# First feed-forward: the norm's root moves from the products into the inputs, which are split anew in place

## The chip, the cores and the metric

The kernel runs on one core of a Trainium2 chip. The metric is the device time of one execution in microseconds. A core has TensorE (PE, with its weight loads PEld), VectorE (DVE), ScalarE (ACT), GpSimd (POOL) and SyncE (SP, which issues most DMAs). Each takes its instructions in order and waits on semaphores where one needs another engine's result.

## The reference

Two layers of a streaming encoder over 1024 prompt frames and 64 sample frames, width 1024, all in fp32. Layer 0 mixes by sliding-window attention, layer 1 by an SSM. Behind each mixer comes a gated feed-forward with a causal convolution of width 3; the change lies in that of layer 0.

```python
def rms_norm(x, g):
    y = x32 * lax.rsqrt(jnp.mean(x32 * x32, axis=-1, keepdims=True) + NORM_EPS) * g
def conv_ffn(h, prev, w_up, conv_w, conv_b, w_down):       # D_FF = 2816
    up = h @ w_up
    full = jnp.concatenate([prev, up], axis=1)
    c = conv_b
    for j in range(CONV_WIDTH):
        c = c + conv_w[j] * full[:, j:j + t]
    return (jax.nn.gelu(c[..., :D_FF]) * c[..., D_FF:]) @ w_down, full[:, -(CONV_WIDTH - 1):]
...
    xp = xp + rms_norm(mp, g_post_mix[i])
    hp = rms_norm(xp, g_pre_ffn[i])
    fp, cpi = conv_ffn(hp, zeros, w_up[i], conv_w[i], conv_b[i], w_down[i])
    xp = xp + rms_norm(fp, g_post_ffn[i])
```

## The kernel before

Activations lie with features on partitions and the 1088 frames along the free dimension, in three blocks `b` of 384, 384 and 320 frames. Each fp32 product is made of three fp32r matmuls: an operand is split into a high part, rounded by a ScalarE copy, and a low part, the remainder by a DVE subtraction (`split`, L458; for weights `split_unit`, L213, into the tiles `whl`). `mm3` (L221 to L225) issues low times high, high times high and high times low.

`post_norm` leaves the residual sum of a block in a tile (`q` behind the attention, `y` elsewhere; the list `ys` in `build`), `pre_norm` (L293) splits that sum times the gain `g`, without the norm's root, into `hh` and `hl` (`h[b][0]`, `h[b][1]`), and puts the root, the same for all features of a frame, into `rb`. So the root is still missing in the products.

`ffn(i, ...)` computes the up-projection in 44 weight tiles of 128 features: tile `f` and tile `KF + f` (KF = 22) belong to one gate. `up_block` (L404) makes one block of a tile in 24 matmuls into one of six PSUM buffers `mm`, and evicts it into the tile's row `u`: by DVE with the factor `rb` (L414, L416), or, with `normed` set, by a ScalarE copy (L411, L412). The second feed-forward (i = 1) uses the copies from its fifth gate on, behind `normed(bs)` (L462), which multiplies `x[b]` in place by gain and root, and new splits of `h`. `conv` (L418) convolves `u` (one step on ScalarE, two on DVE), `gate` (L435) applies GELU, multiplies the two halves (L440) and stores the result to DRAM (`gd`).

The first tiles are computed as `us = up([0, KF, 1])`, block by block over the three; then `gate(0, us)`; then gates 1 to 21. Between the halves of each gate and behind it `aside` counts a turn (44 in all); it advances two side jobs: `sums`, which builds sums of `w_down` (`sums_w`) and of gates (`sums_g`) in the scratch tile `jt`, for the down-projection's block products, and `side`, the preparation of the SSM's tables (`ssm_prep`; its tiles `sm`, `kt`, `w`, and PE's `kps`, `wps` at L1072 and L1083). `jt` and two of the tables use slots that the residual sums held.

Weight tiles are loaded on SP's queue (`raw`, two buffers) and split two units ahead of their use (`AHEAD`) into six slots. The order on each engine is set by a scheduler that goes by priorities and estimated times, not by the order of the code alone; `order` adds fixed precedences on one engine, and `normed`'s products are put behind the last convolution step so far (`last_conv`).

Of the kernel before, what the change touches and what calls it, by code (L numbers as in the profile page):

```python
# [11 lines left out]
AF = mybir.ActivationFunctionType  # L12
# [6 lines left out]
SEQ, DEC, PAST = 1024, 64, 512  # L19
# [3 lines left out]
KF = DFF // P  # L23
# [3 lines left out]
SIDE = 32  # L27

PLAIN = 5
# [14 lines left out]
class Core:  # L44
# [295 lines left out]
    def ffn(self, i, h, rb, after, side=None, beside=lambda: None, x=None, g=None):  # L340

        nc, tc, a = self.nc, self.tc, self.a
# [10 lines left out]
        def sums_w(k):  # L353
            x = (jt[:, :2048] if i == 0 else self.yp.tile([P, 2048], F32, name="jw", tag="ypB", bufs=1)).rearrange("p (c h m) -> p c h m", c=2, h=2)
            Q.dma_start(x, a["w_down"][i, k::KH].rearrange("c p (h m) -> p c h m", h=2))
            yield
            a11, a12, a21, a22 = x[:, 0, 0], x[:, 1, 0], x[:, 0, 1], x[:, 1, 1]
            E.tensor_add(a22, a21, a22)
            E.tensor_sub(a21, a11, a21)
            E.tensor_sub(a11, a22, a11)  # L360
            E.tensor_sub(a12, a12, a11)
            Q.dma_start(sd[:, k], x)
# [14 lines left out]
            Q.dma_start(td[:, k], x)  # L377


        w0 = (PLAIN + 1) * i  # L380
        starts = {2 * (k + w0) + 1: sums_w(k) for k in range(KH)}
        starts.update({2 * (k + KH) + 2: sums_g(k) for k in range(KH)})
        jobs = {}
# [1 line left out]
        def sums(j):  # L385

            for x in jobs.pop(j, []):
                next(x, None)
            if j in starts:
                x = starts[j]  # L390
                next(x)
                jobs[j + 1 + i] = [x]
# [8 lines left out]
        def up_start(m):  # L401
            return self.unit(("w_up", i, m)), u_tile(m)

        def up_block(w, u, b, normed=False):  # L404
            t0, n = BLK[b]
            ps = self.mm_ps()
            for k in range(KD):
                self.mm3(ps[:, :n], w, slice(k * P, (k + 1) * P), h[b][0][:, k], h[b][1][:, k], k == 0, k == KD - 1)
            np_ = min(n, SEQ - t0)
            if normed:  # L410
                nc.scalar.activation(u[:, t0 + 2:t0 + 2 + np_], ps[:, :np_], AF.Copy)  # L411
                nc.scalar.activation(u[:, SEQ + 4:], ps[:, np_:n], AF.Copy)  # L412
                return
            nc.vector.tensor_mul(u[:, t0 + 2:t0 + 2 + np_], rb[:, t0:t0 + np_], ps[:, :np_])  # L414
            if np_ < n:
                nc.vector.tensor_mul(u[:, SEQ + 4:], rb[:, SEQ:], ps[:, np_:n])  # L416

        def conv(m, u):  # L418
# [5 lines left out]
            self.last_conv = nc.vector.scalar_tensor_tensor(t, u[:, 2:T + 4], cw(2, m), t, op0=ALU.mult, op1=ALU.add)  # L424
            return t

        def up(ms):

            wu = {m: up_start(m) for m in ms}
            for b in range(3):  # L430
                for w, u in wu.values():
                    up_block(w, u, b)
            return {m: u for m, (w, u) in wu.items()}

        def gate(f, us):  # L435
            ta = conv(f, us.pop(f) if f in us else up([f])[f])
            nc.scalar.activation(ta, ta, AF.Gelu_apprx_tanh)
            aside()
            tb = conv(KF + f, us.pop(KF + f) if KF + f in us else up([KF + f])[KF + f])
            nc.vector.tensor_mul(ta, ta, tb)  # L440
            Q.dma_start(gd[:, f, :SEQ], ta[:, :SEQ])
            Q.dma_start(gd[:, f, SEQ:], ta[:, SEQ + 2:])
# [3 lines left out]
        def aside():  # L446

            j = next(turns) + 1
            if side is not None and j <= SIDE:
                with self.later(LOW):  # L450
                    next(side, None)
            sums(j - 1)
# [43 lines left out]
        def seven(f, first):  # L496
# [11 lines left out]
            if first:  # L508
                up_block(w, ug, 2)
# [5 lines left out]
            if not first:  # L515
                up_block(w, ug, 2, True)
# [8 lines left out]
            up_block(w, uv, 2, not first)  # L525
            return {f: ug, KF + f: uv}

        us = up([0, KF, 1])
        gate(0, us)
        if i == 0:  # L530
            jt = self.yp.tile([P, 3072], F32, name="jt", tag="ypA", bufs=2)
        else:
            ts_ctx = tc.tile_pool(name="ts", bufs=1)
            ts = ts_ctx.__enter__()
            op = {}
        aside()
        for f in range(1, KF):
            if i == 1 and f == 2:
                normed((0, 1))
            if i == 1 and f == 3:  # L540
                late = input_sums()
            if i == 1 and f == PLAIN - 1:
                us = up([f, KF + f])
                into_place(*late)
                normed((2,))
            if i == 1 and f >= PLAIN:
                us = seven(f, f == PLAIN)
                if f == PLAIN:
                    for j in range(2):
                        split(half(h[2][0], j), half(h[2][1], j), half(x[2], j))  # L550
            if i == 0 and f == KF - 2:
                us = up([f, KF + f, f + 1])
            gate(f, us)
            aside()
# [961 lines left out]
def build(tc, a):  # L1516
    nc = tc.nc
    with ExitStack() as ctx:
        c = Core(ctx, tc, a)
        g = lambda j: c.pp[:, PPO["g"] + j * 8:PPO["g"] + j * 8 + 8]  # L1520
        cols = lambda v: [v[:, :, t0:t0 + n] for t0, n in BLK]
        xin = cols(a["x"])
        xd = [c.dram.tile([P, KD, T], F32, name=f"x{i}") for i in range(3)]
        h = []
        rb = c.t4([P, T], "rb")
        with c.boundary():
            xt = [c.bt(c.yp, b, "y") for b in range(3)]

            last = None
            for b in range(3):  # L1530
                step = 2 if b == 0 else 4
                for k in range(0, KD, step):
                    x = nc.sync.dma_start(xt[b][:, k:k + step], xin[b][:, k:k + step])
                    if last is not None:
                        c.order(x, last)
                    last = x
                    if (b, k) in ((0, 0), (0, 6), (1, 0)):
                        c.load_ahead(1 + len(c.ready))
                        c.order(c.loaded, last)
                        last = c.loaded  # L1540
            c.fill(c.mm_ps("idle"), 14, P)
            c.rest_of_pp()
            for b in range(3):
                h.append(c.pre_norm(xt[b], b, g(0), rb, first=b == 0))
        c.ssm_setup()

        def then(post, xs, xo, pre):

            nxt = [None] * 3
            rb, ys = [], []  # L1550

            def f(b, y):
                ys.append(y)
                c.post_norm(y, b, g(post), xs[b], post != 5 or b == 2, post in (3, 7), xo[b] if pre is None else None,
                            {3: "1111", 7: "0101"}.get(post) if b == 2 else None)()
                if pre == 4:
                    if b == 2:
                        c.ssm_bounce(y, b, [0])
                    c.ssm_norm(y, b)
                    if b == 2:  # L1560
                        c.ssm_bounce(y, b, range(1, 4), dict(c.sq))
                        c.spill = lambda: nc.sync.dma_start(xo[2], y)
                        return
                if pre is not None:
                    nc.sync.dma_start(xo[b], y)
                if pre in (2, 6) and b:
                    second(b - 1)
                    if b == 2:
                        second(2)

            def early():
                for b in range(2):
                    c.ssm_bounce(ys[b], b)

            def second(b):
                if b == 0:
                    rb.append(c.t4([P, T], "rb"))
                nxt[b] = c.pre_norm(ys[b], b, g(pre), rb[0], pre != 6 or b > 0)
            return f, nxt, rb, early, ys
        f, n1, r1, _, _ = then(1, xin, cols(xd[0]), 2)  # L1580
        c.attention(h, rb, f)
        f, _, _, early, _ = then(3, cols(xd[0]), cols(xd[1]), 4)
        c.ffn(0, n1, r1[0], f, c.ssm_prep(), early)
        f, n2, r2, _, ys = then(5, cols(xd[1]), cols(xd[2]), 6)
        c.ssm(f)
        f, _, _, _, _ = then(7, cols(xd[2]), cols(a["o_y"]), None)
        c.ffn(1, n2, r2[0], f, x=ys, g=g(6))
        c.close_ps()
# [21 lines left out]
```

## Time and profile before

| | us |
|---|---|
| runs | 2235.85, 2241.18, 2240.71 |
| median | 2240.71 |
| profiled execution, span | 2241.6 |
| PE busy | 2188.9 |
| DVE busy | 1687.4 |
| ScalarE busy | 1019.1 |
| POOL busy | 414.7 |

The page gives no time for the profiled execution beside its span, which is 0.9 us above the median. Busy times are sums over one engine; they overlap each other. Matmuls are pipelined and their ends are modelled, so a wait of PE is read from gaps and releasers, not from the share alone. A row of a group reads: line, engine, operation, output and inputs, shape, count, busy us in total, mean ns of one, idle time ahead of it and who ended it.

### The profile page before, as it was taken

To read this page: it belongs to the slowest core of one execution; us is meant where nothing else is said; L and a number is where in the kernel's file an instruction comes from. 1 tells how busy PE (TensorE), PEld (TensorE's weight loads), DVE (VectorE), ACT (ScalarE), POOL (GpSimd) and SP (SyncE) were. 2 spreads that over 40 slices of the span, in tenths; PEclk is the share of its full clock that TensorE was granted. 3 is DMA by queue.
4 is the path that set the end of the run, shared out by engine and by line. 5 is a ranking of instruction groups with operands and counts; after the bars stand their busy time and mean duration, and the time that the engine had idled before them with its cause. 6 is when DMAs were issued, how large, how long until landed. Compare 5 with 4: busy or idle time off the path is not lost.

```text
span 2241.6 us, 36077 instructions
## 1 busy us (share of the span) xinstructions
PE 2188.9 (98%) x13875; PEld 2114.0 (94%) x13875; DVE 1687.4 (75%) x2954; ACT 1019.1 (45%) x1839; POOL 414.7 (18%) x474
## 2 busy tenths in 40 slices
PE   9999999999999999999998899999999999999997
PEld 8987789999999999999996699999999999999997
DVE  8687648989877877666768865587997788786754
ACT  5256747422333333455534742263444444455543
POOL 5322004200042323100200034352011111110000
PEclk9999999999999999999999999999999999999999
DMA  5100015656345565887749998751266667678773
GB/s 197 38 22 29 20 62 158 246 184 211 111 136 183 181 192 184 253 298 232 229 147 340 272 295 297 261 167 65 96 217 223 236 237 276 209 269 310 224 243 99
DMA packets 208124, 428.48 MB, mean 191 GB/s; under 512 B 23312, under 2 KB 114224, under 8 KB 205008
## 3 DMA queue, kind: packets, MB, share of 16 engines
q1 hardware_dynamic: 175648, 326.56, 44.3%
q0 software_dynamic: 23984, 95.12, 11.9%
q10 hardware_dynamic: 8320, 4.49, 0.9%
q8 instruction: 109, 1.79, 0.3%
q14 instruction: 63, 0.52, 0.1%
HBM read 297.75 MB, written 128.37 MB: 190 GB/s over the span
## 4 chain that ended last, share of the span: by engine, by line
PE 47%; DMA 6%; DVE 5%; ACT 1%; issue 1%; SPq 1%; POOL 0%; DVEq 0%; ACTq 0%; POOLq 0%
PE mm L225 12%; PE mm L223 12%; PE mm L224 12%; DMA raw<-in_w_down 3%; PE pb L223 1%; PE pb L225 1%; PE pa L224 1%; PE pb L224 1%; PE pa L225 1%; PE pa L223 1%; DVE whl L216 1%; ACT whl L216 1%; DMA yd<-ys 1%; DMA pm<-prm 1%; DVE y L328 0%
## 5 line engine op out<-in xcount | busy, mean ns | idle before, releaser
L223 PE MATMUL mm<-hl,whl 128*128 128x384 f32 (+1 forms) x1960 | 643.4, 329 | 3.8 <-DVE hl L306 3.1
L225 PE MATMUL mm<-hh,whl 128*128 128x384 f32 (+1 forms) x1960 | 641.1, 328 | 2.2 <-DVE whl L216 2.2
L224 PE MATMUL mm<-hh,whl 128*128 128x384 f32 (+1 forms) x1960 | 642.3, 328 | 0.0
L223 PEld LDWEIGHTS mm<-hl,whl 128*128 128x128 f32 x1960 | 368.5, 188 | 6.0 <-DVE hl L306 4.5
L225 PEld LDWEIGHTS mm<-hh,whl 128*128 128x128 f32 x1960 | 368.5, 188 | 2.9 <-DVE whl L216 2.9
L224 PEld LDWEIGHTS mm<-hh,whl 128*128 128x128 f32 x1960 | 368.7, 188 | 0.0
L216 ACT ACTIVATE whl<-raw 128x1024 fp32r<-128x1024 f32 x202 | 212.9, 1058 | 333.4 <-PE mm L225 192.2
L216 DVE TENSOR_TENSOR whl<-raw,whl 128x1024 fp32r<-128x1024 f32 x202 | 254.9, 1264 | 111.2 <-ACT whl L216 110.7
L223 PE MATMUL mm<-gt,whl 128*128 128x384 f32 (+1 forms) x968 | 316.8, 327 | 2.6 <-ACT whl L216 1.7
L225 PE MATMUL mm<-gt,whl 128*128 128x384 f32 (+1 forms) x968 | 315.8, 327 | 0.7 <-DVE whl L216 0.7
L224 PE MATMUL mm<-gt,whl 128*128 128x384 f32 (+1 forms) x968 | 315.9, 327 | 0.0
L223 PEld LDWEIGHTS mm<-gt,whl 128*128 128x128 f32 x968 | 181.7, 188 | 3.2 <-ACT whl L216 1.9
L225 PEld LDWEIGHTS mm<-gt,whl 128*128 128x128 f32 x968 | 181.6, 188 | 1.2 <-DVE whl L216 1.2
L224 PEld LDWEIGHTS mm<-gt,whl 128*128 128x128 f32 x968 | 181.7, 188 | 0.0
L194 DVE TENSOR_TENSOR whl<-raw,whl 128x1024 fp32r<-128x1024 f32 x84 | 96.3, 1153 | 69.2 <-ACT whl L193 68.2
L193 ACT ACTIVATE whl<-raw 128x1024 fp32r<-128x1024 f32 x84 | 82.6, 987 | 115.0 <-DMA raw<-sd 50.2
L423 DVE SCALAR_TENSOR_TENSOR t<-u,ppt,t 128x1090 f32<-128x1090 f32 x88 | 123.6, 1407 | 7.9 <-ACT t L422 7.3
L422 ACT ACTIVATE t<-u,ppt 128x1090 f32<-128x1090 f32 x88 | 114.2, 1298 | 24.4 <-DVE u L521 9.2
L424 DVE SCALAR_TENSOR_TENSOR t<-u,ppt,t 128x1090 f32<-128x1090 f32 x88 | 123.3, 1403 | 0.4
L414 DVE TENSOR_TENSOR u<-rb,mm 128x384 f32<-128x384 f32 (+1 forms) x164 | 80.2, 502 | 20.4 <-PE mm L225 15.7
L566 DVE TENSOR_TENSOR gt<-gr,gt 128x768 fp32r<-128x768 f32 (+2 forms) x106 | 89.9, 879 | 7.1 <-ACT gt L565 6.8
L565 ACT ACTIVATE gt<-gr 128x768 fp32r<-128x768 f32 (+2 forms) x106 | 78.4, 773 | 35.6 <-DMA gr<-gd 24.6
(390 smaller groups left out, 4113.4 us busy)
## 6 DMA issues: line engine op xcount, KB each, us to landing
raw<-in_w_up SPq DMA_DIRECT2D x88, 512.0 KB, 4.2
raw<-in_w_down SPq DMA_DIRECT2D x74, 512.0 KB, 4.4
raw<-sd SPq DMA_DIRECT2D x40, 512.0 KB, 4.6
sj<-in_w_up POOLq DMA_DIRECT2D x68, 256.0 KB, 6.1
su<-sj POOLq DMA_DIRECT2D x34, 512.0 KB, 5.8
raw<-su SPq DMA_DIRECT2D x34, 512.0 KB, 4.7
pm<-prm SPq DMA_DIRECT2D x32, 522.0 KB, 8.6
gr<-td SPq DMA_DIRECT2D x40, 384.0 KB, 5.7
```

Source lines behind the costliest of these rows:

```text
L193: nc.scalar.activation(w[:, 0], raw, AF.Copy)
L194: nc.vector.tensor_sub(w[:, 1], raw, w[:, 0].bitcast(F32))
L216: x = nc.scalar.activation(w[:, 0], raw, AF.Copy), nc.vector.tensor_sub(w[:, 1], raw, w[:, 0].bitcast(F32))
L223: nc.tensor.matmul(out, w[:, 0, sl], xl, start=start, stop=False)
L224: nc.tensor.matmul(out, w[:, 0, sl], xh, start=False, stop=False)
L225: self.last_mm = nc.tensor.matmul(out, w[:, 1, sl], xh, start=False, stop=stop)
L414: nc.vector.tensor_mul(u[:, t0 + 2:t0 + 2 + np_], rb[:, t0:t0 + np_], ps[:, :np_])
L422: nc.scalar.activation(t, u[:, 0:T + 2], AF.Identity, bias=cb(m), scale=cw(0, m))
L423: nc.vector.scalar_tensor_tensor(t, u[:, 1:T + 3], cw(1, m), t, op0=ALU.mult, op1=ALU.add)
L424: self.last_conv = nc.vector.scalar_tensor_tensor(t, u[:, 2:T + 4], cw(2, m), t, op0=ALU.mult, op1=ALU.add)
L565: nc.scalar.activation(x[:, 0, u], raw, AF.Copy)
L566: nc.vector.tensor_sub(x[:, 1, u], raw, x[:, 0, u].bitcast(F32))
```

## The change

In the first feed-forward, behind gate 0, `normed(range(3))` multiplies all three residual sums in place by gain and root (24 DVE instructions). Tile KF + 1 is still computed from the old inputs. Then `resplit` writes `hh` and `hl` of all blocks anew from the multiplied sums, in halves of four features' groups (six ScalarE copies, six DVE subtractions), and from the next tile (2) on products are evicted by ScalarE copies without `rb`. The sums of `w_down` start two turns later, the SSM preparation one turn later, since their scratch tiles come free later.

```diff
-        w0 = (PLAIN + 1) * i
+        w0 = (PLAIN + 1) * i + (i == 0)
...
                 nc.scalar.activation(u[:, t0 + 2:t0 + 2 + np_], ps[:, :np_], AF.Copy)
-                nc.scalar.activation(u[:, SEQ + 4:], ps[:, np_:n], AF.Copy)
+                if np_ < n:
+                    nc.scalar.activation(u[:, SEQ + 4:], ps[:, np_:n], AF.Copy)
...
+        plain = [False]
+
         def up(ms):
             wu = {m: up_start(m) for m in ms}
             for b in range(3):
                 for w, u in wu.values():
-                    up_block(w, u, b)
+                    up_block(w, u, b, plain[0])
...
-            if side is not None and j <= SIDE:
+            if side is not None and 1 < j <= SIDE + 1:
...
+        def resplit():
+            for b in range(3):
+                for j in range(2):
+                    split(half(h[b][0], j), half(h[b][1], j), half(x[b], j))
+
         us = up([0, KF, 1])
         gate(0, us)
         if i == 0:
+            normed(range(3))
+            us.update(up([KF + 1]))
+            resplit()
+            plain[0] = True
             jt = self.yp.tile([P, 3072], F32, name="jt", tag="ypA", bufs=2)
...
-        f, n1, r1, _, _ = then(1, xin, cols(xd[0]), 2)
+        f, n1, r1, _, ys = then(1, xin, cols(xd[0]), 2)
...
-        c.ffn(0, n1, r1[0], f, c.ssm_prep(), early)
+        c.ffn(0, n1, r1[0], f, c.ssm_prep(), early, x=ys, g=g(2))
```

In the changed file the lines of `ffn` stand a little lower: L414 and L416 become L415 and L417, the convolution's DVE steps L423 and L424 become L424 and L425, the gate's product L440 becomes L443, `normed`'s product L470, `split` L462 and L463.

On DVE, at the first gate, before the change: the gate's product (L440) comes behind the sums in `jt`, and behind it the next convolution and the evictions of tile KF + 1 (`sm` belongs to the SSM's tables).

```order
L358 TENSOR_TENSOR jt<-jt 128x512 [waits DMAHW1_49]
L440 TENSOR_TENSOR t<-t 128x1090 [waits DVE_49]
L927 SCALAR_TENSOR_TENSOR sm_4272<-sm_4272 128x32 [waits DVE_49]
L359 TENSOR_TENSOR jt<-jt 128x512 [waits DVE_49]
L423 SCALAR_TENSOR_TENSOR t<-u,ppt,t 128x1090 [waits Activation_49]
L396 MEMSET u 128x2 [waits DVE_49]
L414 TENSOR_TENSOR u<-rb,mm 128x384 x2
L414 TENSOR_TENSOR u<-rb,mm 128x256
L416 TENSOR_TENSOR u<-rb,mm 128x64
```

On DVE at the same place after the change: the 24 products on `q` follow the second convolution step of tile KF, the gate's product stands among them, the evictions of KF + 1 behind them, and then the first four of the new splits.

```order
L470 SCALAR_TENSOR_TENSOR q<-q,ppt,rb 128x384 x8
L470 SCALAR_TENSOR_TENSOR q<-q,ppt,rb 128x384 [waits DMAHW0_49]
L470 SCALAR_TENSOR_TENSOR q<-q,ppt,rb 128x384 x4
L443 TENSOR_TENSOR t<-t 128x1090 [waits DVE_49]
L470 SCALAR_TENSOR_TENSOR q<-q,ppt,rb 128x384 x3
L470 SCALAR_TENSOR_TENSOR q<-q,ppt,rb 128x320 [waits DMAHW4_49]
L470 SCALAR_TENSOR_TENSOR q<-q,ppt,rb 128x320 x7
L396 MEMSET u 128x2
L415 TENSOR_TENSOR u<-rb,mm 128x384 x2
L415 TENSOR_TENSOR u<-rb,mm 128x256
L417 TENSOR_TENSOR u<-rb,mm 128x64
L463 TENSOR_TENSOR hl<-q,hh 128x1536 [waits Activation_49] x4
```

The sums in `jt` have left this place, and the products, and behind the evictions the splits, have come in; the convolution of tile 1 now stands behind the first four splits.

On PE, the end of tile KF + 1 (blocks of 320) and the start of tile 2, after the change; before it the rows are the same, but for the wait on ScalarE in the fourth.

```order
L224 MATMUL mm<-hh,whl 128x320
L225 MATMUL mm<-hh,whl 128x320
L223 MATMUL mm<-hl,whl 128x384 [waits DVE_49,PE_49]
L224 MATMUL mm<-hh,whl 128x384 [waits Activation_49]
L225 MATMUL mm<-hh,whl 128x384
```

Nothing moved on PE: tile 2 follows tile KF + 1 as before. Its first two matmuls now read the operands that DVE and ScalarE write anew.

On ScalarE, a little later, before the change (`cst` keeps the last columns of `u`):

```order
L398 COPY u<-ppt 128x2
L419 COPY cst<-u 128x4 [waits DVE_49]
L422 ACTIVATE t<-u,ppt 128x1090 [waits DVE_49,Activation_49]
L398 COPY u<-ppt 128x2 [waits DVE_49]
L216 ACTIVATE whl<-raw 128x1024 [waits DMAHW2_49,PE_49]
L437 ACTIVATE t<-t 128x1090 [waits DVE_49]
```

And after it, for tile 2:

```order
L411 ACTIVATE u<-mm 128x384 [waits PE_49] x2
L440 ACTIVATE t<-t 128x1090 [waits DVE_49]
L411 ACTIVATE u<-mm 128x256 [waits PE_49]
L413 ACTIVATE u<-mm 128x64
L216 ACTIVATE whl<-raw 128x1024 [waits DMAHW3_49]
L420 COPY cst<-u 128x4 [waits Activation_49]
```

The evictions have come to ScalarE, between GELU and the weight split.

## The prediction

> **What bounds the kernel now.** First the page's busy times and its chain, then the windows of the first feed-forward's up-projection (some 376 to 892 us), then what PE waits for there, then the timeline at the place that the change rewrites.
>
> ```profile
> PE 2188.9 (98%) x13875; PEld 2114.0 (94%) x13875; DVE 1687.4 (75%) x2954; ACT 1019.1 (45%) x1839; POOL 414.7 (18%) x474
> ...
> PE 47%; DMA 6%; DVE 5%; ACT 1%; issue 1%; SPq 1%; POOL 0%; DVEq 0%; ACTq 0%; POOLq 0%
> ```
>
> PE is busy in 2188.9 of 2241.6 us: 52.7 us of idle time in the whole program. An edit that only shortens DVE's or ScalarE's work can win back some of these and nothing else; an edit that makes PE wait adds to them in full. Now the stage by windows (columns: PE, weight loads, DVE, ACT, POOL, granted clock, DMA share, GB/s); the last row is from the second feed-forward, where part of the products already leave PSUM as plain copies on ScalarE.
>
> ```profile
> core 0: us, PE busy (x) PEld busy (x) DVE busy (x) ACT busy (x) POOL busy (x), PEclk, DMA share, GB/s
> 420.00:450.00 30.00, 29.93 (x184) 29.67 (x183) 28.70 (x63) 14.67 (x20) 0.00 (x0) 1.00 0.67 239
> 450.00:500.00 50.00, 50.00 (x304) 50.00 (x303) 42.26 (x118) 13.30 (x21) 0.00 (x0) 1.00 0.54 192
> 550.00:600.00 50.00, 50.00 (x305) 50.00 (x304) 46.45 (x136) 14.80 (x22) 0.00 (x0) 1.00 0.44 149
> 650.00:700.00 50.00, 47.80 (x305) 47.20 (x304) 40.51 (x56) 19.61 (x29) 18.73 (x13) 1.00 0.48 154
> 750.00:800.00 50.00, 47.72 (x296) 47.16 (x295) 37.39 (x52) 18.42 (x24) 13.81 (x9) 1.00 0.63 198
> 850.00:900.00 50.00, 47.01 (x288) 46.07 (x287) 36.27 (x55) 16.82 (x25) 22.02 (x15) 1.00 0.55 172
> ...
> 1650.00:1700.00 50.00, 50.00 (x304) 50.00 (x303) 41.74 (x56) 21.98 (x38) 6.44 (x12) 1.00 0.69 244
> ```
>
> DVE is the fullest helper (46.45 of 50 us at 550), yet PE does not stop there: 304 matmuls in 50 us whether DVE is busy for 42 or for 46. PE loses 2 to 3 us in three later windows. Its waits, first from 380 to 640 us, then from 640 to 900 us (total us, times, longest):
>
> ```profile
> PE mm L223 <- DVE hl L306: 3.1, 3, 1.6
> ...
> PE wps L1083 <- DVE kt L1077: 5.1, 4, 1.6
> PE wps L1083 <- DVE w L897: 2.4, 3, 1.1
> ```
>
> So 3.1 + 7.5 = 10.6 us are all that a lighter DVE can give back in this stage.
>
> **The change: PE must wait for the new split.** The new parts are put between tile KF+1 and tile 2, the fourth and the fifth weight tile. PE's order is the same as before: KF+1's last block, then tile 2's first block. But tile 2 now reads inputs that are written anew in place, so it waits for them. Before, tile 2 followed at once:
>
> ```profile
> 423.30 0.31 PE L225 MATMUL mm<-hh,whl 128*128 128x320 f32 x1
> 423.45 0.33 PE L223 MATMUL mm<-hl,whl 128*128 128x384 f32 x1
> ```
>
> When are the new inputs there? DVE's order in the changed program is: the convolution of tile KF, the 24 in-place products with root and gain, among them the first gate's product, the four scaled evictions of KF+1, then the first split. The convolution of KF is held by ScalarE, which in order waits for a weight slot, loads its table, applies GELU and only then starts KF's convolution (L422); these rows have the same order and waits in the new program.
>
> ```profile
> 423.65 1.06 ACT L216 ACTIVATE whl<-raw 128x1024 fp32r<-128x1024 f32 x1 [1.69 <-PE mm L225]
> 424.73 1.28 ACT L437 ACT_TABLE_LOAD   x1
> 426.02 1.12 ACT L437 ACTIVATE t<-t 128x1090 f32<-128x1090 f32 x1
> 427.04 1.28 ACT L422 ACTIVATE t<-u,ppt 128x1090 f32<-128x1090 f32 x1
> ...
> 428.36 1.35 DVE L423 SCALAR_TENSOR_TENSOR t<-u,ppt,t 128x1090 f32<-128x1090 f32 x1 [0.79 <-ACT t L422]
> ...
> 429.75 1.35 DVE L424 SCALAR_TENSOR_TENSOR t<-u,ppt,t 128x1090 f32<-128x1090 f32 x1
> ```
>
> DVE is thus free for the new work at 429.75 + 1.35 = 431.1. Its prices, from the groups by shape (busy us in total, mean ns); L467 and L460 are the same operations of the same shapes in the second feed-forward:
>
> ```profile
> L440 DVE TENSOR_TENSOR t<-t 128x1090 f32<-128x1090 f32 x44 | 59.9, 1361 | 0.1
> L414 DVE TENSOR_TENSOR u<-rb,mm 128x384 f32<-128x384 f32 x108 | 57.8, 547 | 7.9 <-PE mm L225 7.8
> L414 DVE TENSOR_TENSOR u<-rb,mm 128x256 f32<-128x256 f32 x56 | 23.2, 414 | 12.5 <-PE mm L225 7.8 <-ACT rb L308 4.7
> L416 DVE TENSOR_TENSOR u<-rb,mm 128x64 f32<-128x64 f32 x56 | 11.9, 212 | 0.0
> L467 DVE SCALAR_TENSOR_TENSOR y<-y,ppt,rb 128x384 f32<-128x384 f32 x16 | 8.6, 617 | 0.0
> L460 DVE TENSOR_TENSOR hl<-y,hh 128x1536 fp32r<-128x1536 f32 x4 | 7.0, 1749 | 1.2 <-ACT hh L459 1.2
> L467 DVE SCALAR_TENSOR_TENSOR y<-y,ppt,rb 128x320 f32<-128x320 f32 x8 | 3.8, 542 | 0.0
> L460 DVE TENSOR_TENSOR hl<-y,hh 128x1280 fp32r<-128x1280 f32 x2 | 3.0, 1488 | 0.3 <-ACT hh L459 0.3
> ```
>
> - In-place products: 8.6 + 3.8 = 12.4 us.
> - The gate's product between them: 59.9 / 44 = 1.4 us.
> - KF+1's evictions: 2 x 57.8/108 + 23.2/56 + 11.9/56 = 1.7 us.
> - The first split: 1.75 us.
>
> 431.1 + 12.4 + 1.4 + 1.7 + 1.75 = 448.3, against 423.45: PE stands for **24.9 us**. ScalarE's half of the split (L459) needs only the products, so it is done while DVE still multiplies. From there PE needs 12 x 50/304 = 2.0 us for each half of a block and DVE makes a half in 1.75: the second half and the second block follow in time, and for the third (two pieces of 1.5 us behind one convolution step) I allow 0.3 us, inside the rounding. Behind the waiting matmul stands PE's whole remaining program; DVE and ScalarE are late with convolutions of tiles 1 and KF+1 at that time, which only the gate's stores wait for. Bounds of the stall: 22 (neighbours overlap more tightly than the group rows say) to 27 (semaphores, a later convolution).
>
> Does PE come back at full speed? The rows for a restart (PEclk is the third column from the end):
>
> ```profile
> 10.00:12.00 2.00, 1.85 (x7) 1.85 (x8) 2.00 (x5) 1.70 (x3) 0.00 (x0) 0.62 1.06 400
> 12.00:14.00 2.00, 2.00 (x8) 2.00 (x7) 2.00 (x3) 1.27 (x3) 1.37 (x1) 0.52 1.04 413
> ...
> 1194.00:1196.00 2.00, 1.68 (x8) 1.26 (x8) 0.46 (x3) 1.56 (x4) 0.41 (x6) 0.73 1.09 343
> 1196.00:1198.00 2.00, 1.56 (x13) 1.29 (x14) 0.61 (x3) 0.36 (x3) 0.00 (x0) 0.50 1.05 401
> 1198.00:1200.00 2.00, 2.00 (x13) 1.64 (x10) 1.27 (x4) 0.00 (x0) 0.19 (x1) 0.50 1.03 410
> 1200.00:1202.00 2.00, 2.00 (x17) 1.74 (x17) 1.93 (x5) 0.00 (x0) 0.00 (x0) 0.56 1.01 384
> ```
>
> Lost there: 2 x (0.38 + 0.48) = 1.7 us at the program's start, 2 x (0.27 + 0.5 + 0.5 + 0.44) = 3.4 us at 1194. I take **1.7**, the row with the same dense matmuls, with 0 and 3.4 as ends. The Trainium skill, "TensorE: Matmul & The Clock Gate", Part 1, says that an idle window of about 3.4 us halves the clock and that the window runs free, so that half speed lasts between one and two windows: by that an estimate of 2.6 us, and a sum 0.9 higher.
>
> **What the change takes away.** From tile 2 on, 40 tiles are evicted by ScalarE: DVE loses 40 x 1.7 = 68 us of work, ScalarE gains
>
> ```profile
> L411 ACT ACTIVATE u<-mm 128x256 f32<-128x256 f32 x32 | 12.3, 385 | 72.0 <-PE mm L225 72.0
> L510 ACT ACTIVATE u<-mm 128x384 f32<-128x384 f32 x17 | 8.3, 487 | 0.0
> L412 ACT ACTIVATE u<-mm 128x64 f32<-128x64 f32 x32 | 7.0, 218 | 0.0
> ```
>
> 40 x (2 x 0.487 + 0.385 + 0.218) = 63 us, for which it has room (20 of 50 us busy). While PE never stops, this is worth nothing; where PE waits for DVE (7.5 us) some comes back. In the new order the evictions ahead of `kt` are gone, but the convolutions and the sums in `jt` stay ahead of it. Ends 0 and 7.5; I take half, **3.8**. The sums' first pieces no longer stand among the splits near 400 us; of the 3.1 us there I take **1.0** (0 to 3.1), since POOL's and ScalarE's shares of that split stay.
>
> The moved steps: the sums of `w_down` start two turns later, their loads and stores on SP's queue with them (22 DMAs, issued between the same weight loads); the last now ends at turn 24, where the first sums of `g` begin, and products read them only after turn 44. The SSM tables start one turn later and are wanted only by the mixer behind this feed-forward. Both: 0, with the remaining 20 turns of PE work as cover; SP's weight loads run two units ahead of PE. If that cover failed, PE would wait for a weight load at the seams of tiles.
>
> Sum: 2241.6 + 24.9 + 1.7 - 3.8 - 1.0 = 2263.4. The span is 0.9 above the median of the three runs (2240.71), so on their scale **2262.5 us**, 1.0% slower. What a measurement of this kernel can tell from no change is about 0.3%, 6.7 us.
>
> **Rivals.**
>
> 1. *DVE's load paces PE without showing as a wait, and its relief decides (faster).* The place is 450 to 640 us, the price up to 1.7 us for each of 40 tiles: 2241.6 + 26.6 - 68 = 2200. It decides once it is over 26.6 / 40 = 0.67 us per tile. Against it: 304 matmuls per 50 us at 42.26, at 46.45, and at 41.74 with ScalarE evicting (1650). The Trainium skill, "Perfetto Trace Analysis", "Optimizing Scalar/DVE Operations", says that work of a saturated DVE may be worth moving to ScalarE; its section on the most-contended engine judges PE by weight-load time, which is 50.00 of 50 here, and so sides with the trace. 0.04.
> 2. *The stall is given back later (no change).* The `w_down` loads are 3% of the chain; did they run by their own clock, they would get ahead during the stall, and the end stay near 2240. Against it: the splits of loaded weights wait for PE to free a slot,
>
> ```profile
> ACT whl L216 <- PE mm L225: 192.2, 53, 9.5
> ```
>
> so loads move with PE. 0.05.
>
> 3. *ScalarE's queue holds PE up.* Evictions wait for PE, and weight splits and convolutions queue behind them. If a third of each tile's 1.58 us of evictions came late enough to stop PE, that were 40 x 0.5 = 20 us: 2282. Against it: 50.00 of 50 us in the window at 1650. 0.08.
>
> **How the numbers follow.** My forecast has 0.83. Its own bounds: 2240.7 + 22 - 10.6 = 2252 and 2240.7 + 27 + 3.4 = 2271; half of the small rivals' weight lies outside on either side, so the range is 2251 to 2272. Faster 0.04 (the first rival), same 0.05 (the second), slower 0.91.
>
> **What would show it.** In the profile after: PE idle once for 22 to 27 us near 423 us, released by DVE's split of `hl`; the granted clock near 0.5 for some 3 us behind it; 24 in-place products of 12 us in one row on DVE just ahead; DVE's busy time lower by 68 - 22 us, ScalarE's higher by about 70; `kt` waits near 4 us. The forecast is wrong if PE's gap is under 15 us, if the matmuls per 50 us rise from 304, or if PE waits for ScalarE tile after tile.

## The result, and the profile after

The changed kernel takes 2267.3 us (median; 2262.3 to 2270.8) against 2240.5 for the kernel before, a ratio of 1.0118 (95% interval 1.0101 to 1.0135). It is slower by 27 us. The profiled execution's span is 2268.2 us, 26.6 above that of before, so the two profiles can be compared step by step. The medians below leave out two executions that took far longer than all others (3611 us in `fill_short`, 4860 us of the kernel before on the chip of `pair_spread`). From the page after, busy times and the chain by engine:

```profile
PE 2195.9 (97%) x13875; PEld 2121.6 (94%) x13875; DVE 1663.7 (73%) x2824; ACT 1077.4 (47%) x2005; POOL 414.6 (18%) x474
PE 79%; DVE 9%; DMA 7%; ACT 3%; issue 2%; SPq 1%; POOL 0%; ACTq 0%; DVEq 0%; POOLq 0%
```

DVE has 23.7 us less to do and ScalarE 58.3 more, as the change says, and the program is longer. PE's waits from 380 to 950 us, after (total us, times, longest); line numbers of the changed kernel stand up to 13 above those of before:

```profile
PE mm L223 <- DVE hl L463: 24.1, 1, 24.1
PE wps L1096 <- DVE u L396: 4.2, 3, 1.5
PE mm L223 <- DVE hl L306: 1.0, 1, 1.0
PE wps L1096 <- DVE w L910: 0.4, 1, 0.4
```

One wait is new: PE stands still for 24.1 us until DVE has split the new inputs. DVE's timeline at that place (start, us, line, operation), and PE's first matmul behind it:

```profile
426.85 1.35 DVE L424 SCALAR_TENSOR_TENSOR t<-u,ppt,t 128x1090 f32<-128x1090 f32 x1 [1.23 <-ACT t L423]
...
428.24 1.35 DVE L425 SCALAR_TENSOR_TENSOR t<-u,ppt,t 128x1090 f32<-128x1090 f32 x1
429.51 6.96 DVE L470 SCALAR_TENSOR_TENSOR q<-q,ppt,rb 128x384 f32<-128x384 f32 x13
436.39 1.29 DVE L443 TENSOR_TENSOR t<-t 128x1090 f32<-128x1090 f32 x1
437.59 5.37 DVE L470 SCALAR_TENSOR_TENSOR q<-q,ppt,rb 128x384 f32<-128x384 f32 x11
442.89 0.55 DVE L415 TENSOR_TENSOR u<-rb,mm 128x384 f32<-128x384 f32 x1
...
444.28 6.76 DVE L463 TENSOR_TENSOR hl<-q,hh 128x1536 fp32r<-128x1536 f32 x4
```

```profile
446.18 0.66 PE L223 MATMUL mm<-hl,whl 128*128 128x384 f32 x1 [24.07 <-DVE hl L463]
446.63 0.53 PE L224 MATMUL mm<-hh,whl 128*128 128x384 f32 x1
446.95 0.53 PE L225 MATMUL mm<-hh,whl 128*128 128x384 f32 x1
...
451.53 0.34 PE L225 MATMUL mm<-hh,whl 128*128 128x384 f32 x1
```

The convolution of gate 0 ends at 429.6, the 24 products run to 443.0 with the gate's product between them, tile KF + 1 is evicted, and the first split (1.75 us) ends at 446.0, just ahead of PE's start. The matmuls behind it begin 0.32 us apart in place of 0.17, until 451.1. The windows after, there and right behind (columns as in the prediction, PEclk third from the end):

```profile
420.00:450.00 30.00, 5.93 (x27) 5.69 (x26) 28.49 (x51) 16.08 (x15) 0.00 (x0) 0.62 0.17 56
450.00:500.00 50.00, 50.00 (x301) 50.00 (x300) 45.72 (x127) 18.51 (x35) 0.00 (x0) 0.99 0.56 189
```

15 matmuls at 0.15 us more each are 2.2 us of clock. From 500 to 600 us there are 304 matmuls in each 50 us, as before.

Where the rest comes in is seen from the starts of the same instructions in each profile (us; of the down-projection the first row on L225, the third matmul of `mm3`):

| profile of | first product of the down-projection | first SSM product | last SSM product | SSM stage | span |
|---|---|---|---|---|---|
| before | 930.1 | 1196.7 | 1298.3 | 101.6 | 2241.6 |
| after | 951.7 | 1221.1 | 1326.2 | 105.1 | 2268.2 |
| shift | +21.6 | +24.4 | +27.9 | +3.5 | +26.6 |

At the down-projection the balance is closed to about 1 us: waits 30.0 against 11.0, 2.2 us of clock behind the stop and 1.7 at 395 us make 22.9, and the shift is 21.6 (21.9 from a start that is 0.3 earlier). Another 6.3 us arise between there and the end of the SSM stage, where the edit changes no line, and 1.3 are won back later. Of the 6.3, 2.8 come ahead of the SSM stage: PE's waits there are 9.1 us against 8.5, and the clock is at 0.50 once more than before (from 1185.1 us for 3.4 us, 1.7 us if PE is busy throughout).

### The profile page after: what moved, and what is told of

Same layout as the page of the kernel before. It is cut to its first block, busy times and chain, and to the rows that moved or that the text cites. A ratio compares the mean times of both kernels' runs of the same rounds, so it can differ in the third digit from the quotient of the medians.

```text
span 2268.2 us, 36074 instructions
## 1 busy us (share of the span) xinstructions
PE 2195.9 (97%) x13875; PEld 2121.6 (94%) x13875; DVE 1663.7 (73%) x2824; ACT 1077.4 (47%) x2005; POOL 414.6 (18%) x474
## 4 chain that ended last, share of the span: by engine, by line
PE 79%; DVE 9%; DMA 7%; ACT 3%; issue 2%; SPq 1%; POOL 0%; ACTq 0%; DVEq 0%; POOLq 0%
PE mm L223 20%; PE mm L225 20%; PE mm L224 20%; PE po L818 2%; PE pb L223 1%; PE pb L225 1%; PE pa L224 1%; PE pb L224 1%; PE pa L225 1%; PE pa L223 1%; DMA raw<-in_w_down 1%; PE tps L811 1%; PE sps L788 1%; DVE whl L216 1%; DMA yd<-ys 1%
## 5 line engine op out<-in xcount | busy, mean ns | idle before, releaser
L223 PE MATMUL mm<-hl,whl 128*128 128x384 f32 (+1 forms) x1960 | 644.6, 329 | 25.5 <-DVE hl L463 24.1
L225 PE MATMUL mm<-hh,whl 128*128 128x384 f32 (+1 forms) x1960 | 642.9, 329 | 2.3 <-DVE whl L216 2.3
L216 DVE TENSOR_TENSOR whl<-raw,whl 128x1024 fp32r<-128x1024 f32 x202 | 256.1, 1270 | 165.4 <-ACT whl L216 164.6
L225 PEld LDWEIGHTS mm<-hh,whl 128*128 128x128 f32 x1960 | 369.7, 189 | 3.0 <-DVE whl L216 2.9
L225 PE MATMUL mm<-gt,whl 128*128 128x384 f32 (+1 forms) x968 | 316.0, 327 | 0.7 <-DVE whl L216 0.7
L225 PEld LDWEIGHTS mm<-gt,whl 128*128 128x128 f32 x968 | 182.1, 188 | 1.1 <-DVE whl L216 1.0
L411 ACT ACTIVATE u<-mm 128x384 f32<-128x384 f32 (+1 forms) x152 | 66.6, 439 | 236.4 <-PE mm L225 236.2
L424 DVE SCALAR_TENSOR_TENSOR t<-u,ppt,t 128x1090 f32<-128x1090 f32 x88 | 124.6, 1418 | 9.2 <-ACT t L423 8.1
L423 ACT ACTIVATE t<-u,ppt 128x1090 f32<-128x1090 f32 x88 | 114.7, 1304 | 23.1 <-DVE u L524 10.3
L425 DVE SCALAR_TENSOR_TENSOR t<-u,ppt,t 128x1090 f32<-128x1090 f32 x88 | 121.9, 1386 | 0.6
```

Source lines behind the costliest of these rows:

```text
L216: x = nc.scalar.activation(w[:, 0], raw, AF.Copy), nc.vector.tensor_sub(w[:, 1], raw, w[:, 0].bitcast(F32))
L223: nc.tensor.matmul(out, w[:, 0, sl], xl, start=start, stop=False)
L225: self.last_mm = nc.tensor.matmul(out, w[:, 1, sl], xh, start=False, stop=stop)
L423: nc.scalar.activation(t, u[:, 0:T + 2], AF.Identity, bias=cb(m), scale=cw(0, m))
L424: nc.vector.scalar_tensor_tensor(t, u[:, 1:T + 3], cw(1, m), t, op0=ALU.mult, op1=ALU.add)
```

## The experiments

Time is the median, the ratio is to the kernel before on the same chip (2237.3 to 2240.3 us there).

**The copies on ScalarE without new inputs (`relief`).** Edit, on the kernel before (`plain` is handed to `up_block` as in the change):

```diff
+            us.update(up([KF + 1]))
+            plain[0] = True          # ScalarE copies from tile 2 on; no normed, no resplit
```

> The kernel before, with ScalarE copying the products of up-projection tiles 2 to 42 (81 blocks' worth and more) out of PSUM unscaled from the second gate on; no root is put into the inputs and nothing is split anew, so those products lack the norm's root. PE therefore never stops for the inputs. Theory (the stop is the loss, the relief is small): the waits on the SSM side products fall from 7.5 to about 4.5 us, ratio 0.9985, about 2237 us (2234 to 2241). Rival, DVE's load was pacing PE: 30 us or more faster, 2210 us or less. Rival, ScalarE's queue in order holds the copies and with them PE: slower by 5 to 20 us, 2246 to 2260 us.

2256.8 us, 1.0069 (1.0055 to 1.0084): 16 us slower with no stop in it. The theory's 2237 us is missed by 20 us; the last rival's range is met, though not by its road, for PE waits for none of the copies. PE's waits from 380 to 950 us:

```profile
PE wps L1088 <- DVE w L902: 9.8, 3, 3.8
PE mm L223 <- DVE gt L571: 4.9, 1, 4.9
```

DVE has less work, and PE waits more for DVE: 9.8 us for `w`, a side product of the SSM preparation (2.4 before), and 4.9 us for `gt`, an operand of the down-projection (none before). All waits together are 18.2 us against 11.0; some 5 us at half clock behind them come on top, which closes the 12.1 us by which the down-projection begins later here. DVE's timeline ahead of one such wait shows what DVE does meanwhile:

```profile
769.23 1.23 DVE L216 TENSOR_TENSOR whl<-raw,whl 128x1024 fp32r<-128x1024 f32 x1 [1.17 <-ACT whl L216]
771.15 0.69 DVE L899 TENSOR_TENSOR w<-m 128x512 f32<-128x512 f32 x1 [0.70 <-DMA prm<-oc]
771.76 1.35 DVE L424 SCALAR_TENSOR_TENSOR t<-u,ppt,t 128x1090 f32<-128x1090 f32 x1
773.02 0.69 DVE L900 TENSOR_TENSOR m<-tq,tp 128x512 f32<-128x512 f32 x1
773.62 0.68 DVE L901 TENSOR_TENSOR m<-tq,tp 128x512 f32<-128x512 f32 x1
774.23 0.55 DVE L370 TENSOR_TENSOR jt<-jt 128x384 f32<-128x384 f32 x1
774.70 1.35 DVE L425 SCALAR_TENSOR_TENSOR t<-u,ppt,t 128x1090 f32<-128x1090 f32 x1
775.96 0.69 DVE L902 TENSOR_TENSOR w<-m 128x512 f32<-128x512 f32 x1
```

It waits at a weight split for ScalarE's half, and between the last pieces of `w` stand side sums and a convolution; PE starts at 776.70, 3.82 us late. The same wait in the group of weight splits over the whole program (x202 | busy, mean ns | idle ahead of it), of before, of after and of this run:

```profile
L216 DVE TENSOR_TENSOR whl<-raw,whl 128x1024 fp32r<-128x1024 f32 x202 | 254.9, 1264 | 111.2 <-ACT whl L216 110.7
```

```profile
L216 DVE TENSOR_TENSOR whl<-raw,whl 128x1024 fp32r<-128x1024 f32 x202 | 256.1, 1270 | 165.4 <-ACT whl L216 164.6
```

```profile
L216 DVE TENSOR_TENSOR whl<-raw,whl 128x1024 fp32r<-128x1024 f32 x202 | 254.1, 1262 | 153.3 <-ACT whl L216 152.8
```

What DVE saves on evictions shows up for the larger part as idle time ahead of these splits, ended by ScalarE's halves: 110.7 us before, 164.6 after. One explanation of the 16 us is that side work stands badly in DVE's queue against PE's, since the scheduler set a new order for all of it. That can be tested, because the change also moves the side work.

**The same with the change's two moves (`relief_moved`), with one of them (`relief_sums`, `relief_side`), and the moves alone (`moves`).**

```diff
-        w0 = (PLAIN + 1) * i
+        w0 = (PLAIN + 1) * i + (i == 0)          # sums: relief_moved, relief_sums, moves
-            if side is not None and j <= SIDE:
+            if side is not None and 1 < j <= SIDE + 1:   # side: relief_moved, relief_side, moves
```

> The run with ScalarE's plain copies and no new inputs (the root is left out of the later tiles), and beside it the change's other part: side sums two turns later, the SSM preparation one turn later. Theory, the 16 us of that run were waits of PE for side work that the scheduler set badly against DVE (9.8 us for w alone, and 8 us of clock behind such waits), and with the side work where the change puts it these fall to the changed kernel's 4.6 us: 2234 to 2242 us, ratio 0.997 to 1.001. Rival, ScalarE's copies themselves cost: 2250 us or more, as without the moves.

> The kernel before with the two moves alone: side sums of weights two turns later, the SSM preparation one turn later. Theory: nothing of note, 2237 to 2243 us, ratio 0.999 to 1.001; the waits for hl near 400 us fall from 3.1 to 1 us, those on the side products stay within 3 us of their 7.5. Rival, the moves alone open or close waits of 5 us and more: outside 2235 to 2246 us.

> The run with ScalarE's plain copies and no new inputs, 16 us slower than the kernel before; of the two moves that took these 16 us away together, the one of the side sums (two turns later) alone. If it is the order of jt sums between DVE's side work that decides: 2236 to 2243 us. If it is the SSM preparation's place: 2250 to 2258 us as without any move.

> The same run with the other move alone, the SSM preparation one turn later. If its place decides: 2236 to 2243 us. If the side sums' place decides: 2250 to 2258 us. If both runs lie between, the two share the 16 us.

| run | time | ratio (95%) | PE waits for SSM side products, 380 to 950 us |
|---|---|---|---|
| relief | 2256.8 | 1.0069 (1.0055 to 1.0084) | 11.4 |
| relief_side | 2250.9 | 1.0058 (1.0042 to 1.0074) | 12.2 |
| relief_sums | 2243.2 | 1.0026 (1.0017 to 1.0036) | 7.4 |
| relief_moved | 2239.3 | 1.0001 (0.9992 to 1.0010) | 5.0 |
| moves | 2238.8 | 1.0004 (0.9994 to 1.0014) | 2.0 |

The rows behind the last two numbers, of `relief_moved` and of `moves`:

```profile
PE wps L1088 <- DVE u L396: 3.9, 3, 1.5
PE mm L223 <- DVE hl L306: 3.1, 3, 1.6
PE wps L1088 <- DVE w L902: 1.1, 2, 0.6
```

```profile
PE mm L223 <- DVE hl L306: 3.1, 3, 1.6
PE wps L1083 <- DVE kt L1077: 1.5, 1, 1.5
PE wps L1083 <- DVE w L897: 0.5, 1, 0.5
```

With both moves the 16 us are gone; the copies then give what they cost, to 0.1%. The side sums' place is the larger part of it, and neither move does it alone (`relief_sums` came out just above its 2243 us, `relief_side` at the low end of the range for "the side sums decide"). Two readings follow. The relief of DVE is worth nothing when the stop is left out, which settles the first rival. And the side waits fall to 2.0 us by the moves alone, with DVE evicting as before, more than the 3 us that I had allowed, though by the end those moves gain nothing: `moves` starts its down-projection at 923.4, 6.7 us ahead of before, and its SSM stage 0.8 us behind it. Most of what takes this back stands at one place of the down-projection, where before has no wait: PE waits 2.96 us until 1022.8 for `y` (L616), and the clock is at 0.50 from there to 1028.9, some 3 us more. The profiled execution is the longest of the 12 of `moves`, 5 us over their median, so this loss may not be in the others.

**The stop without the copies (`stall`), and without the products (`noprod`).**

```diff
 stall:             resplit()
-            plain[0] = True
 noprod:
-            normed(range(3))
             us.update(up([KF + 1]))
```

> The changed kernel, but DVE goes on with its scaled copies out of PSUM, as before: the root is counted twice in the later tiles. The products and the new split stay, and so does the stop. Theory: the stop alone carries the loss, 24 us and 2 us of clock behind it, and the 4 to 5 us that come later, in the SSM stage, stay too, since the instructions stand there in the changed kernel's order; less 2 us of waits near 400 us: +27 to +31 us, 2268 to 2272 us, ratio 1.012 to 1.014. If the copies on ScalarE are a part of the loss: below +22 us. If the relief was worth much and hid a larger loss: above +40 us.

> The changed kernel without the 24 products that put gain and root into the inputs (both are missing from the later tiles); the inputs are split anew as they stand. Theory (the stop is DVE's work in a row): 12.4 us of products fall out of the stop, which measures 10 to 13 us in place of 24.1; time 12 us below the changed kernel, 2253 to 2258 us, ratio about 1.0065. Rival, ScalarE's splits or its table load set the end of the stop: it stays above 18 us.

`stall`: 2264.8 us, 1.0115 (1.0093 to 1.0138), a little under its 2268; the wait is 24.1 us again. So the new inputs carry the loss, 24.5 us here of 26.8 in the changed kernel, with or without ScalarE's copies. `noprod`: 2245.7 us, 1.0029 (1.0016 to 1.0041), and here the time came out 7 us below the expected range, and the stop was not shorter but gone. DVE's splits and PE's largest wait in it:

```profile
414.52 1.75 DVE L463 TENSOR_TENSOR hl<-q,hh 128x1536 fp32r<-128x1536 f32 x1
...
416.51 1.75 DVE L463 TENSOR_TENSOR hl<-q,hh 128x1536 fp32r<-128x1536 f32 x1
...
421.06 1.75 DVE L463 TENSOR_TENSOR hl<-q,hh 128x1536 fp32r<-128x1536 f32 x1
...
424.08 3.15 DVE L463 TENSOR_TENSOR hl<-q,hh 128x1536 fp32r<-128x1536 f32 x2
```

```profile
PE mm L223 <- DVE u L415: 5.2, 1, 5.2
```

I had only taken the products out of the row and left the rest where it stood. But it was the products, placed behind the convolution of gate 0, that held the splits back: without them each half of a block can be split once tile KF + 1 has read it, the first at 414.5 us (a stop that was only 12 us shorter would have ended at 434), and PE does not stop at tile 2 at all. It stops 12 us later, at 433.7, for a late eviction.

**The same computation without the stop (`pair`, `pair_spread`).** Tiles 2 and KF + 2 are made from the old inputs too, so that products and splits run beside 24 us of PE work (edits written short):

```diff
-            normed(range(3))
             us.update(up([KF + 1]))
-            resplit()
+            normed(range(3)); us.update(up([2, KF + 2])); resplit()    # pair
+            us.update(up([2, KF + 2]))                                 # pair_spread:
+            for b in range(3): normed([b]); resplit(b)                 # products behind KF+1's evictions
```

> The changed kernel, but tiles 2 and KF+2 are also computed from the old inputs, block by block, before the inputs are split anew, so that the 24 products run while PE works, and each block's split runs while PE is in the next block. Theory: the stop falls from 24.1 to under 2 us, its clock loss with it, and the instructions of the SSM stage stand in the order of the kernel before, so the later 4 to 5 us go as well: 2233 to 2240 us, ratio 0.997 to 1.000 against the kernel before. Rival, the lost time comes back elsewhere (loads of the side sums that wait for the inputs' buffers, DVE overfull from 425 to 475 us): 2245 to 2258 us. Rival, the relief is large once there is no stop: 2215 us or less.

> As the run with tiles 2 and KF+2 on the old inputs, but the 24 products stand behind the evictions of tile KF+1, and block by block between the evictions of tiles 2 and KF+2 and the splits, so that no eviction waits behind 7 us of products. In that run PE lost 3.6 us near 438 us and 1.6 us near 477 us to late evictions, and some 3 us of clock behind them. Theory: these 8 us go, 2240 to 2247 us, ratio 0.999 to 1.003. Rival, the loss sits in the later waits on the SSM side products (9 us in both) and not here: 2249 us or more.

2251.7 us, 1.0058 (1.0042 to 1.0074), and 2250.5, 1.0057 (1.0043 to 1.0072). Both theories are missed (2240 and 2247 us at most), and both rivals' ranges are met. Both programs beat the changed kernel by 13 us by the ratios, 15 by the medians, and neither comes back to the kernel before. The largest waits in `pair`, 380 to 950 us:

```profile
PE mm L223 <- DVE u L415: 3.6, 1, 3.6
PE wps L1097 <- DVE u L396: 2.9, 2, 1.5
PE wps L1097 <- DVE kt L1091: 2.1, 1, 2.1
PE kps L1086 <- DVE ct L1060: 1.9, 1, 1.9
PE wps L1097 <- DVE w L911: 1.8, 1, 1.8
PE mm L223 <- ACT u L411: 1.6, 1, 1.6
```

The 24.1 us are gone; in their place stand many small waits, 15.8 us against 11.0 before, and 5.1 us lost to half clock behind them where before lost none. `pair_spread` does away with the eviction wait of 3.6 us, but waits 3.1 us for three of the splits, 3.2 us for a copy of ScalarE's at 477, and 5.0 us for `ct` and `w`; its profiled execution (2258.1 us) is the longest of six, so its waits may be larger than usual. DVE is busy for 46.6 of the 50 us from 425 to 475 in `pair`, with 22 us of products and splits more to do than before, and PE waits for it at several later places. Even the program without any new inputs is only level with before (`relief_moved`), so nothing here points to a version that would beat the kernel before.

**The clock behind the stop (`fill`, `fill_short`).** Matmuls on constants in PE's queue, where it otherwise stands:

```diff
             us.update(up([KF + 1]))
+            self.fill(self.mm_ps("idle"), 36, 512, self.last_mm)    # fill; 27 in fill_short
             resplit()
```

> The changed kernel with 36 matmuls of 512 columns on constants in PE's queue between tile KF+1 and tile 2, where PE otherwise stands still; nobody reads them. They take 36 x 0.59 = 21 us of the stop of 24.1. Theory: the clock stays at full speed, and tile 2's first 15 matmuls take 0.174 us each in place of 0.32, so 2 us less: 2262 to 2266 us, granted clock 0.95 or more from 446 to 451 us. Rival, the half speed there is not from PE's standing still: 0.6 again. Rival, the filling delays tile 2: 2268 us or more.

> As the run with filling matmuls in the stop, but 27 of them: in that run each took two passes of 0.43 us, 30.5 us in all, so that the last ended 6.2 us after the inputs were there. 27 x 0.85 = 23 us should end at 445, a microsecond before the inputs. Theory: granted clock 1.00 from 420 to 455 us, tile 2's matmuls at full pitch from the start, and the down-projection's first product comes 2 us earlier than in the changed kernel (949 to 950 us in place of 951.7); the rest as there, since the SSM stage's order is the changed kernel's: 2263 to 2267 us. Rival, the half speed cost nothing that counted: 951 to 952 us again.

`fill`: 2269.4 us, 1.0138 (1.0120 to 1.0157). I had priced a filling matmul at one pass; each took two (72 records 0.43 us apart for 36 matmuls), and the last ended 6 us after the inputs were there, so the last rival's range is met. `fill_short`: 2271.3 us, 1.0137 (1.0113 to 1.0161), above its 2267; its runs spread from 2261 to 2276 us, and the profiled one (2263.9) lies near their low end. Its windows, beside those of after shown above:

```profile
420.00:450.00 30.00, 29.10 (x92) 15.87 (x91) 28.34 (x52) 16.27 (x18) 0.00 (x0) 1.00 0.16 54
450.00:500.00 50.00, 50.00 (x305) 50.00 (x304) 44.26 (x117) 18.80 (x36) 0.00 (x0) 1.00 0.56 191
```

The clock stays at 1.00, and tile 2 runs at full pitch behind its first matmul. From that matmul to the down-projection it takes 503.3 us (447.3 to 950.6) where after takes 505.5 (446.2 to 951.7): 2.3 us won, the 2.2 of the clock. The half speed is from standing still. In the time of the whole it did not show; the spread of the runs is larger than what was sought.

**The SSM stage (`ssm_order`).** ScalarE's and SyncE's orders there differ between before and after, though no line of that stage was touched:

```diff
+                    if kt in (1, 2): self.order(x, self.last_u)     # the load of yf behind that of U
+                if qs[0] in (4, 6): scs(x)                          # sc behind rd, as before
```

> The changed kernel with the SSM stage's instructions on ScalarE and SyncE put back into the order in which they stand in the kernel before (order edges alone; one memset on GpSimd still stands one row later); the stop for the inputs stays. Theory, the changed order there costs about 3 us: the SSM stage from its first to its last product takes 101 to 103 us in place of 105.1 (101.6 in the kernel before), time 2262 to 2265 us. Rival, the 3 us are run to run: 104 to 106 us there, 2266 to 2269 us.

2264.1 us, 1.0114 (1.0099 to 1.0129). The stage takes 101.1 us in its profile. PE's waits in it, of after and then of this run:

```profile
PE p L1272 <- DVE wk L1320: 5.2, 2, 4.5
PE p L1332 <- ACT ys L1346: 4.4, 1, 4.4
```

```profile
PE p L1345 <- DVE wk L1330: 4.2, 5, 2.1
PE p L1272 <- DMA pm<-prm: 3.9, 4, 1.9
```

The single long wait for ScalarE's `ys` stands in the three profiles with after's order (4.4 us in after, 3.1 in `stall`, 4.0 in `noprod`; in the last a few instructions on ScalarE stand otherwise), where the stage takes 103.1 to 105.1 us, and in none of the eleven others (100.2 to 102.5). So some 3 us go with that order, by the profiles; the 3 us between the medians of `ssm_order` and after are not resolved by their intervals. The cause is not shown: `fill_short` has after's order on ScalarE and SyncE (but for one DMA issue) and another on GpSimd, and takes 100.2; `ssm_order` has after's order on GpSimd, and takes 101.1. By these two profiles neither part of the order does it alone; whether the three queues together do, or something that the order does not fix, stays open.

## Why the prediction was right, and where it was not

2262.5 us was forecast (2251 to 2272), 2267.3 measured. By its steps:

- **The stop, 24.9 us**: 24.1 measured, and in the forecast's order: convolution, 12.3 us of products, the gate's product, evictions, split. It began 1.3 us earlier than I had put it (422.1), and the convolution ended 1.5 us earlier (429.6). `stall` shows that it carries the loss, `noprod` that the products in it are what opens it.
- **The clock, 1.7 us**: 2.2 us; half speed lasted 4.9 us of PE's work (446.2 to 451.1), and `fill_short` shows the cause. By the Trainium skill ("TensorE: Matmul & The Clock Gate", Part 1), with its window of 3413 ns that runs free, the estimate was 2.6 us; the trace agrees in that the 4.9 us lie between one window and two.
- **Side waits, -3.8**: 7.5 became 4.6, -2.9. The size was near by luck, the cause wrong: I gave it to DVE's relief. `moves` brings the waits down to 2.0 with no relief, and `relief` brings them up to 11.4 with all of it.
- **Waits for `hl` near 400 us, -1.0**: 3.1 became 1.0, -2.1. That the side sums left from there is not why: in `moves` and `relief_moved`, where they left too, it is 3.1. It falls in every program with new inputs; the order of that stretch changes with them.
- **Moved steps, 0**: 0 alone (`moves`, 1.0004), but 16 us beside ScalarE's copies. The cover that I named, turns of PE work, was not the point; by the waits for `w`, what counts is where the side work falls in DVE's queue against PE's.
- **Nothing behind the feed-forward**: this is the step that failed. Between the down-projection and the end of the SSM stage 6.3 us came on top, and 1.3 went again: 5.0 in all, against the 4.8 us by which the profiled shift of 26.6 exceeds the forecast's 21.8. Some 3 us of it go with the new order in the SSM stage, up to 1.7 with one more stretch of half clock ahead of it; what sets either off stays open.
- **DVE's busy time, 46 lower**: 23.7 (ScalarE's, about 70 higher: 58.3). Evictions, products and splits have the forecast's rows (scaled evictions of the larger pieces 80.2 to 20.7 us, products 12.3, splits 9.6); their sum doesn't give the fall of the engine's busy time. Part of the difference is the measure: neighbouring rows overlap, and busy time counts an overlap once. Summed over all rows of the two traces DVE's durations fall by 39.0 us (1858.8 to 1819.9), of which 23.7 are left in the busy time. The other 7 us were not traced.
- **Rivals**: the first (relief decides) falls by `relief_moved`, which takes the relief and is level with before. The second (given back later) did not come: the time grew later. The third (ScalarE's queue holds PE) is right in a smaller form in other orders: 3.2 us for one copy in `pair_spread`, and DVE's 54 us more of idle time ahead of ScalarE's splits; in the changed kernel itself PE waits for ScalarE's copies nowhere in that stage.

## What to carry to other kernels

Moving work off a full helper engine pays only if the bounding engine waits for that engine; here DVE stood idle for 54 us more ahead of ScalarE's splits, and PE saw nothing of the gain. A step that rewrites an operand in place stops the reader for the whole chain of work on the way, so look first at what its first instruction is ordered behind: without the 24 products the splits cost PE no stop. And where a scheduler sets the order, an edit need not stay local: two moves were worth 0 or 16 us depending on what stood beside them, and a stage that was not touched took 3 us more in the profile.

## What the runs showed of the hardware

Short waits of PE can cost as much in clock as in time. In `pair` PE waited 1.9 us until 674.5 for `ct`; the windows behind (PE busy, PEclk, DMA share, GB/s):

```profile
674.00:675.00 1.00, 0.49 (x3) 1.00 0.38 137
675.00:676.00 1.00, 1.00 (x6) 0.61 1.07 381
676.00:677.00 1.00, 1.00 (x4) 0.50 0.02 6
677.00:678.00 1.00, 1.00 (x4) 0.50 0.00 0
678.00:679.00 1.00, 1.00 (x7) 0.69 0.00 0
```

That is 0.39 + 0.5 + 0.5 + 0.31 = 1.7 us lost, half of the 3.4 us that the dip lasted, behind a wait of only 1.9 us. From 2 us ahead of the SSM stage to its end the clock is at 0.50 for 10.2 us in before and 23.9 in after, three and seven times 3.4. Half of that is an upper bound of the loss, since PE stands idle for some of it; the stage is 3.5 us longer. A wait of about a microsecond brought one in after at 395 us, and three such waits (1.6 us the longest) brought none in before at 397 to 405. The Trainium skill ("TensorE: Matmul & The Clock Gate", Part 1) has a free-running window of 3413 ns; the length of these dips agrees with it, and that a similar wait brings a dip once and not another time would fit a window that runs free. Its advice to allow no idle gaps over some 3 us between matmuls ("Why this matters for your kernels") is not strict enough here: the wait of 1.9 us was followed by a dip.
